# A one-core decoder layer: feed-forward loads begun at the end of the attention scores, their first splits ahead of the last output product's, token transposes further back

## The chip, the cores and the metric

The kernel runs on one core of a Trainium2 chip. The metric is the time of the program on the device in microseconds (us). Before the change three runs took 573.92 to 576.64 us, with a median of 574.91.

The engines of the core are TensorE (PE in the profile, its weight loads PEld), VectorE (DVE), ScalarE (ACT), GpSimd (POOL) and SyncE (SP). Each works through its own list of instructions in order, and semaphores tie the lists together. Transfers are issued from the lists of SP and POOL; those that add to what lies in memory are issued from POOL.

## The reference

One decoder layer on 512 tokens of width 1024, in float32: a norm, one input projection, three groups of heads (dilated attention with 6 heads, gated linear attention with 4, block-sparse attention with 6), an output projection with a residual, a second norm, a feed-forward part of width 4096 with a squared ReLU and a residual, and a final norm.

```python
def hybrid_layer(x, norm1_w, w_in, w_a2, b_a, gla_norm_w, w_out, norm2_w, w_ff1, w_ff2, rel_bias):
    Bsz, S, _ = x.shape
    h = rmsnorm(x, norm1_w)
    proj = h @ w_in
    aq, ak, av, bq, bk, bv, br, ba, cq, ck, cv = jnp.split(proj, list(np.cumsum(IN_SIZES)[:-1]), axis=-1)
    ...
    y_a = dilated_attention(heads(aq, A_HEADS), heads(ak, A_HEADS), heads(av, A_HEADS), bias_a)
    y_b = gla(heads(bq, B_HEADS), heads(bk, B_HEADS), heads(bv, B_HEADS), br, ba, w_a2, b_a, gla_norm_w)
    y_c = moba_attention(heads(cq, C_HEADS), heads(ck, C_HEADS), heads(cv, C_HEADS), bias_c)
    mix = jnp.concatenate([y_a.reshape(Bsz, S, A_WIDTH), y_b, y_c.reshape(Bsz, S, C_WIDTH)], axis=-1)
    x = x + mix @ w_out

    h2 = rmsnorm(x, norm2_w)
    x = x + jnp.square(jax.nn.relu(h2 @ w_ff1)) @ w_ff2
    return x

def reference(x, norm1_w, w_in, gla_w_a2, gla_b_a, gla_norm_w, w_out, norm2_w, w_ff1, w_ff2, rel_bias, final_norm_w):
    for i in range(DEPTH):
        x = hybrid_layer(x, norm1_w[i], w_in[i], gla_w_a2[i], gla_b_a[i], gla_norm_w[i], w_out[i],
                         norm2_w[i], w_ff1[i], w_ff2[i], rel_bias)
    return rmsnorm(x, final_norm_w)
```

With 512 tokens and blocks of 256, the block-sparse heads attend to all past keys, so both attention groups end as full causal scores with their own biases and masks.

## The kernel before, in words

**Arithmetic.** A float32 weight tile `wraw` (128 x 1024, 512 KB) is split in two: `wh`, rounded to the format that TensorE multiplies fast (a copy on ACT), and `wl`, the rest (a subtraction on DVE). Activations are split in the same way. A product is then three matmuls: high by high, high by low, low by high.

**Block products.** The output projection and the feed-forward matrices are multiplied in 2 x 2 blocks by seven block products instead of eight (numbers 0 to 6, executed in the order 0, 1, 3, 5, 2, 4, 6). Products 0 and 1 take blocks as they are; the others take sums and differences of blocks. Their results gather in accumulators X (0, 2, 4, 6), Y (1) and Z (3, 5). Each product of the output projection has two halves of 128 tokens (q = 0, 1) with 12 matmuls of 512 columns each. Each product of a feed-forward unit has two halves of 24 matmuls of 256 columns. There are four chunks of the hidden width, each with a unit for w_ff1 (accumulators f1X, f1Y, f1Z) and one for w_ff2 (f2X, f2Y, f2Z).

**Sums of weights.** The blocks of weights that a product needs are summed on the way in: a plain transfer from SP brings one block, and an adding transfer from POOL (`o_plus`, `plus`) puts the next on top. A product's buffer is often the buffer of an earlier product with one more block, and then the add has to wait until the earlier product's split has read it.

**Stages.** Projections and gated linear attention come first, then scores, softmax (`P`), transposes of `P` (`ptp`, `turn`) and values (`po`) by pairs of heads. As values end, `mix_out` splits them and makes the sums that the output projection multiplies (`ms`, `mh`, `ml`). `out_proj` runs the seven products; `o_add` adds each to the residual `x3` on DVE. When both halves of the width of a tile of 128 tokens are there (tiles 0 and 1 after product 2, tiles 2 and 3 after product 6), `x2_done` makes the reciprocal of the norm (`junk`, `m`, `tmp`, `y`), `y_out` scales the tile (`y0`), transposes it on TensorE (`yps`, eight 128 x 128 transposes in two accumulator banks), and scales it into `yf`; `y_parts` forms sums (`ys`) and splits (`yp`), which are the operands of the first feed-forward unit.

**What sets the order.** Every part is a Python generator (a stream) that hands out one instruction at a time. `Plan.run` keeps its own estimate of each engine's time and, of all streams, issues the instruction that could start first; ties go by the stream's priority (`prio`, the lower number first). ("take", name) and ("give", name) count buffers: `big` is a buffer of 4 KB a partition, `w` the right to split one more weight pair, `raw`, `rawo` and `raw2` the rights to load. ("wait", key) and `fire(key)` tie streams. What comes out is a fixed list for each engine; the waits on the chip then follow from the data. So an edit of one stream's rights shifts the order of others too.

In the kernel before, `fetch_o` loads product 6 of the output projection as a sum of its own: for each of its two weight tiles (ip = 0, 1) one plain transfer and three adding ones. `fetch_ff` and `cut_ff`, which load and split the feed-forward's weights, start when the last score transposes have been planned, and `cut_ff` waits until all of the output projection's splits have been planned ("o cut"). The first unit's splits are done in halves of 512 columns.

Of the kernel before, what the change touches and what calls it, by code (L numbers as in the profile page):

```python
# [100 lines left out]
class Plan:  # L101
# [48 lines left out]
    def run(self):  # L150
        while self.streams:
            cand, moved = None, False
            for st in list(self.streams):
                while True:
                    if st["item"] is None:
                        try:
                            moved = True
                            self.now = st["sent"] if st["sent"] is not None else st["at"]
                            st["item"] = st["gen"].send(st["sent"])
                        except StopIteration:  # L160
                            self.streams.remove(st)
                            break
                    it = st["item"]
                    if isinstance(it, tuple):
                        kind, key = it
                        if kind == "prio":
                            st["prio"] = key
                        elif kind == "wait":
                            if key not in self.done:
                                break  # L170
                            st["at"] = max(st["at"], self.done[key])
                        else:
                            if not self.free[key]:
                                break
                            t = min(self.free[key])
                            self.free[key].remove(t)
                            st["at"] = max(st["at"], t)
                        st["sent"], st["item"] = st["at"], None
                        continue
                    o = self.best(st)  # L180
                    first = o[0] if isinstance(o, list) else o
                    t = max(self.start(x, st["at"]) for x in (o if isinstance(o, list) else [o]))
                    if cand is None or (t, st["prio"], st["n"]) < cand[:3]:
                        cand = (t, st["prio"], st["n"], st, o)
                    break
            if cand is None:
                if moved:
                    continue
                if self.streams:
                    raise RuntimeError("streams wait for ever")  # L190
                return
            t, _, _, st, o = cand
            end = 0.0
            for x in o if isinstance(o, list) else [o]:
                end = max(end, self.issue(x, t))
            st["item"], st["sent"] = None, end
# [3 lines left out]
def hybrid_block_kernel(ctx: ExitStack, tc: tile.TileContext, xT_d, x_d, w0_d, wv_d, wqk_d, wo_d, w1_d, w2_d,  # L200
# [220 lines left out]
                fire(("x3", t, half))  # L421

    def fetch_o():
        for n, q, more in ((0, (0, 0), None), (1, (1, 0), None), (5, (1, 1), None), (4, (0, 1), ((1, 1),)),
                           (6, (1, 0), ((0, 0), (0, 1), (1, 1)))):
            for ip in range(2):
                yield ("take", "rawo")
                yield ("take", "big")
# [6 lines left out]

    def cut_o():
        for n in O_ORDER:
            for ip in range(2):
                yield ("wait", ("oB", n, ip))
                t = VB["o", n, ip]  # L440
                yield from parts(("o", n, ip), t)
                if n in (0, 3):
                    spawn(o_plus(2 if n else 3, ip, t, ((1 if n else 0, 1),)), 3)
                else:
                    give("rawo")
                    give("big")

        fire("o cut")

    XS = {}  # L450
    units = [(i, c) for c in range(NC) for i in (1, 2)]
# [106 lines left out]
            yield ("take", "w")  # L558

    def cut_ff():  # L560
        yield ("wait", "o cut")
        for u in units:
            for o, (n, *_) in enumerate(PRODUCTS):
                if u == units[0] or u == units[1]:
                    yield ("prio", 0.5 if u == units[0] else 3)
                if u == units[-1]:
# [671 lines left out]
    def y_out(t, half, y):  # L1238
        y0 = slot("y0")
        yield Any(DVE.tensor_scalar(y0, x3[t, half], y, None, op0=OP.mult), ACT.activation(y0, x3[t, half], AF.Copy, scale=y))  # L1240
        r = "og"[half] if t % 2 else "pt"
        yield ("take", r)
        pt = bank(r, "yps")
# [63 lines left out]
    def out_proj():  # L1307
# [39 lines left out]
        for n in O_ORDER:  # L1347
            if n == 1:
                yield ("wait", "scores")
                for q in range(2):  # L1350
                    yield from part(n, q, (0, 1, 2))
                yield ("wait", "turns")
                for q in range(2):
                    yield from part(3, q, (0, 1, 2))
                spawn(fetch_ff(), 4)
                spawn(cut_ff(), 3)
                spawn(y_parts(), 0.4)
            for q in range(2):
                yield from part(n, q, (3,) if n in (1, 3) else (0, 1, 2, 3))
            give_w()  # L1360
            give_w()
            if n in (2, 3):
                give("big")
                give("big")
            if n == 2:
                give("w")
                give("w")
            give("raw2")

    hq = {}  # L1370
# [343 lines left out]
```

## Time and profile before

| | before |
|---|---|
| median of 3 runs | 574.91 us (573.92 to 576.64) |
| the profiled execution | 574.53 us, span 572.8 us |
| PE busy | 555.9 us, 97% of the span |
| DVE busy | 480.9 us, 84% |
| ACT busy | 372.4 us, 65% |
| POOL busy | 71.1 us, 12% |
| bytes moved | 99.73 MB, 173 GB/s over the span |
| mean granted clock of TensorE | 0.996 |
| output projection on TensorE | 191.4 to 244.8 us |
| first feed-forward unit begins | 245.0 us |

Reading it: the profiled execution took 574.53 us in all, 1.7 us more than its span from the first to the last instruction. Matmuls on TensorE overlap, so its busy time is not its work; what tells of a loss is an idle time before an instruction and what ended it. An engine off the critical path may idle at no cost.

### The profile page before, as it was taken

The page shows a single profiled execution, that of the slowest core. Times are in us where ns is not written, and L with a number is a line of the kernel's source. Part 1 is how long each engine was busy: PE and PEld are TensorE (multiplying, and loading weights), DVE is VectorE, ACT ScalarE, POOL GpSimd, SP SyncE. Part 2 cuts the span into 40 slices and gives each one's busy share as a digit, 9 for nine tenths or more (in the row PEclk, how much of TensorE's full clock was granted, in tenths as well). Part 3 has the DMA queues.
Part 4 walks back from the last instruction along what each step waited for, and adds up shares of the span by engine and source line. Part 5 has one row for each costly group of instructions (what it writes and reads, how often), then busy time and mean ns, then how long its engine had stood idle before and what let it go on. Part 6 is the DMA issues. An engine that isn't in the chain of part 4 may idle for free.

```text
span 572.8 us, 9467 instructions
## 1 busy us (share of the span) xinstructions
PE 555.9 (97%) x3513; PEld 478.6 (84%) x3513; DVE 480.9 (84%) x879; ACT 372.4 (65%) x662; POOL 71.1 (12%) x93
## 2 busy tenths in 40 slices
PE   9999999999999999998999999999999999999994
PEld 8977887886786767788988899988999888999883
DVE  5899899977876988799799996799967799867993
ACT  6755644795865775788785466855467655579543
POOL 4012110001011011101212002020020110112101
PEclk9999999999999999999999999999999999999998
DMA  8944694396087549965988529787278594395812
GB/s 287 405 116 114 112 239 107 111 376 124 5 165 195 153 119 271 243 213 129 229 241 166 171 95 243 239 147 217 92 160 278 133 195 157 96 215 112 147 54 94
DMA packets 30813, 99.73 MB, mean 174 GB/s; under 512 B 3744, under 2 KB 3786, under 8 KB 30768
## 3 DMA queue, kind: packets, MB, share of 16 engines
q0 software_dynamic: 10032, 35.62, 34.4%
q1 hardware_dynamic: 20448, 63.25, 31.7%
q8 instruction: 27, 0.44, 0.3%
q10 hardware_dynamic: 288, 0.27, 0.1%
q14 instruction: 18, 0.15, 0.1%
HBM read 97.00 MB, written 2.13 MB: 173 GB/s over the span
## 4 chain that ended last, share of the span: by engine, by line
PE 85%; DVE 8%; ACT 3%; issue 1%; DMA 1%; SPq 0%; DVEq 0%; ACTq 0%
PE f2X L129 15%; PE f1X L129 15%; PE qkps L129 11%; PE f2Z L129 8%; PE f1Z L129 7%; PE vps L129 6%; PE ops L129 4%; PE f2Y L129 4%; PE f1Y L129 3%; PE sps L129 2%; PE po L129 2%; PE ptp L129 2%; DVE wl L129 2%; PE av L129 1%; DVE yf L129 1%; PE lp L129 1%
## 5 line engine op out<-in xcount | busy, mean ns | idle before, releaser
L129 DVE TENSOR_TENSOR wl<-wraw,wh 128x1024 fp32r<-128x1024 f32 (+2 forms) x174 | 191.3, 1109 | 36.0 <-ACT wh L129 35.8
L129 ACT ACTIVATE wh<-wraw 128x1024 fp32r<-128x1024 f32 (+2 forms) x173 | 164.3, 965 | 54.7 <-DVE x L129 9.7
L129 PE MATMUL f1X<-yp,wh 128*128 128x256 f32 x512 | 92.7, 283 | 0.0
L129 PEld LDWEIGHTS f1X<-yp,wh 128*128 128x128 f32 x512 | 80.1, 192 | 0.3
L129 POOL DMA_DIRECT2D wraw<-in_w x46 | 40.4, 952 | 273.8 <-DVE wl L129 205.2
L129 PE MATMUL f1X<-yp,wl 128*128 128x256 f32 x256 | 72.4, 283 | 0.0
L129 PE MATMUL f2X<-wh,Al 128*128 128x512 f32 (+1 forms) x132 | 50.5, 383 | 0.0
L129 PE MATMUL f2X<-wh,Ah 128*128 128x512 f32 (+1 forms) x132 | 50.5, 383 | 0.0
L129 PE MATMUL f2X<-wl,Ah 128*128 128x512 f32 (+1 forms) x132 | 50.5, 383 | 0.0
L129 PEld LDWEIGHTS f1X<-yp,wl 128*128 128x128 f32 x256 | 49.1, 192 | 0.0
L129 PE MATMUL f1Z<-yp,wh 128*128 128x256 f32 x256 | 46.3, 283 | 0.0
L129 PE MATMUL qkps<-xh,wh 128*128 128x512 f32 x96 | 40.8, 425 | 1.6 <-DVE vals L129 1.2
L129 ACT ACTIVATE h<-h 128x512 f32<-128x512 f32 x56 | 34.7, 625 | 11.5 <-DVE h L129 11.0
L129 PEld LDWEIGHTS f1Z<-yp,wh 128*128 128x128 f32 x256 | 39.9, 192 | 0.0
L129 ACT ACTIVATE Ah<-h 128x512 fp32r<-128x512 f32 x40 | 24.2, 620 | 22.2 <-DVE h L129 22.2
L129 PE MATMUL f1Z<-yp,wl 128*128 128x256 f32 x128 | 36.4, 284 | 1.8 <-DVE wl L129 1.8
L129 PE MATMUL qkps<-xh,wl 128*128 128x512 f32 x96 | 37.6, 392 | 0.0
L129 PE MATMUL qkps<-xl,wh 128*128 128x512 f32 x96 | 37.5, 391 | 0.0
L129 ACT ACTIVATE P<-P,mn 128x512 f32<-128x512 f32 (+3 forms) x48 | 26.5, 554 | 14.3 <-DVE mn L129 14.1
L129 PEld LDWEIGHTS f2X<-wl,Ah 128*128 128x128 f32 x132 | 24.8, 188 | 4.8
L129 PEld LDWEIGHTS f2X<-wh,Al 128*128 128x128 f32 x132 | 24.8, 188 | 4.8
L129 PEld LDWEIGHTS f2X<-wh,Ah 128*128 128x128 f32 x132 | 24.8, 188 | 4.7
(261 smaller groups left out, 1229.9 us busy)
## 6 DMA issues: line engine op xcount, KB each, us to landing
wraw<-in_w SPq DMA_DIRECT2D x66, 512.0 KB, 5.7
wraw<-in_w POOLq DMA_DIRECT2D x46, 512.0 KB, 6.4
wraw<-in_wqk SPq DMA_DIRECT2D x12, 512.0 KB, 6.5
wraw<-in_wo POOLq DMA_DIRECT2D x12, 512.0 KB, 7.4
wraw<-in_wv SPq DMA_DIRECT2D x10, 512.0 KB, 7.1
wraw<-in_wo SPq DMA_DIRECT2D x10, 512.0 KB, 6.2
wraw<-in_wv POOLq DMA_DIRECT2D x8, 512.0 KB, 5.8
nb<-tab SPq DMA_DIRECT2D x12, 256.0 KB, 4.8
```

Of the source, the lines that this page charges most:

```text
L129: getattr(getattr(self.nc, op.eng), op.method)(*op.args, **op.kw)
```

## The change

Four things change.

- `fetch_o` no longer loads product 6. In `cut_o`, product 2's buffer, once split, gets block (1, 0) added and becomes product 6's (`o_plus(6, ...)`), as product 0's already became product 3's and product 3's product 2's.
- `fetch_ff` and `cut_ff` are started as soon as the scores are planned, ahead of product 1. `cut_ff` waits for the split of output product 4 before it splits feed-forward product 0, and for that of output product 6 before feed-forward product 3. So the splits of feed-forward products 0 and 1 may come ahead of product 6's, which has the priority 0.4.
- Two rights to split (`w`) are given back after the last score transposes, not after product 2.
- The planner learns an item ("delay", t), which moves a stream's own earliest time on by t in the planner's estimate and issues nothing. `y_out` uses it with 2.0 between the scaled tile and its transposes.

```diff
--- before.py
+++ after.py
@@ -165,6 +165,8 @@
                         kind, key = it
                         if kind == "prio":
                             st["prio"] = key
+                        elif kind == "delay":
+                            st["at"] += key
                         elif kind == "wait":
                             if key not in self.done:
                                 break
@@ -421,8 +423,7 @@
                 fire(("x3", t, half))
 
     def fetch_o():
-        for n, q, more in ((0, (0, 0), None), (1, (1, 0), None), (5, (1, 1), None), (4, (0, 1), ((1, 1),)),
-                           (6, (1, 0), ((0, 0), (0, 1), (1, 1)))):
+        for n, q, more in ((0, (0, 0), None), (1, (1, 0), None), (5, (1, 1), None), (4, (0, 1), ((1, 1),))):
             for ip in range(2):
                 yield ("take", "rawo")
                 yield ("take", "big")
@@ -435,17 +436,19 @@
 
     def cut_o():
         for n in O_ORDER:
+            if n == 6:
+                yield ("prio", 0.4)
             for ip in range(2):
                 yield ("wait", ("oB", n, ip))
                 t = VB["o", n, ip]
                 yield from parts(("o", n, ip), t)
-                if n in (0, 3):
-                    spawn(o_plus(2 if n else 3, ip, t, ((1 if n else 0, 1),)), 3)
+                if n in (0, 3, 2):
+                    m, q = {0: (3, (0, 1)), 3: (2, (1, 1)), 2: (6, (1, 0))}[n]
+                    spawn(o_plus(m, ip, t, (q,)), 3)
                 else:
                     give("rawo")
                     give("big")
-
-        fire("o cut")
+            fire(("o cut", n))
 
     XS = {}
     units = [(i, c) for c in range(NC) for i in (1, 2)]
@@ -558,9 +561,10 @@
             yield ("take", "w")
 
     def cut_ff():
-        yield ("wait", "o cut")
         for u in units:
             for o, (n, *_) in enumerate(PRODUCTS):
+                if u == units[0] and o in (0, 2):
+                    yield ("wait", ("o cut", 6 if o else 4))
                 if u == units[0] or u == units[1]:
                     yield ("prio", 0.5 if u == units[0] else 3)
                 if u == units[-1]:
@@ -1238,6 +1242,7 @@
     def y_out(t, half, y):
         y0 = slot("y0")
         yield Any(DVE.tensor_scalar(y0, x3[t, half], y, None, op0=OP.mult), ACT.activation(y0, x3[t, half], AF.Copy, scale=y))
+        yield ("delay", 2.0)
         r = "og"[half] if t % 2 else "pt"
         yield ("take", r)
         pt = bank(r, "yps")
@@ -1347,13 +1352,15 @@
         for n in O_ORDER:
             if n == 1:
                 yield ("wait", "scores")
+                spawn(fetch_ff(), 4)
+                spawn(cut_ff(), 3)
                 for q in range(2):
                     yield from part(n, q, (0, 1, 2))
                 yield ("wait", "turns")
+                give("w")
+                give("w")
                 for q in range(2):
                     yield from part(3, q, (0, 1, 2))
-                spawn(fetch_ff(), 4)
-                spawn(cut_ff(), 3)
                 spawn(y_parts(), 0.4)
             for q in range(2):
                 yield from part(n, q, (3,) if n in (1, 3) else (0, 1, 2, 3))
@@ -1362,9 +1369,6 @@
             if n in (2, 3):
                 give("big")
                 give("big")
-            if n == 2:
-                give("w")
-                give("w")
             give("raw2")
 
     hq = {}
```

On TensorE, where product 2 of the output projection ends and product 4 runs, the first token tile's transposes stood here before (`ops_2354` and `ops_2492` are the two halves of accumulator X):

```order
L129 MATMUL ops_2492<-wl_2726,ms_2186 128x512
L129 MATMUL ops_2354<-wh_2732,ms_2196 128x512
L129 MATMUL ops_2354<-wh_2732,ms_2198 128x512
L129 MATMUL ops_2354<-wl_2733,ms_2196 128x512
L129 MATMUL yps_2807<-cst_80,y0_2804 128x128 x4
L129 MATMUL yps_2809<-cst_80,y0_2805 128x128 x4
```

and now stand here, with `ops_2386` and `ops_2461` as the two halves:

```order
L129 MATMUL ops_2386<-wl_2740,ms_2185 128x512
L129 MATMUL ops_2461<-wh_2724,ms_2184 128x512
L129 MATMUL ops_2461<-wh_2724,ms_2186 128x512
L129 MATMUL ops_2461<-wl_2725,ms_2184 128x512
...
L129 MATMUL yps_2837<-cst_80,y0_2831 128x128 x4
L129 MATMUL yps_2840<-cst_80,y0_2832 128x128 x4
```

The transposes moved from behind the first 3 matmuls of product 4 to behind 18 of its 24. Those of the second tile stood behind 15 matmuls of product 4 and now stand behind all of it and six of product 6.

On DVE, at the same place, before (`x3` is the residual, `wraw_2120` product 6's first weight tile):

```order
L129 TENSOR_TENSOR wl_2759<-wraw_2120,wh_2758 128x1024
L129 TENSOR_TENSOR x3_2142<-x3_2142,ops_2354 128x512
L129 SCALAR_TENSOR_TENSOR m_2689<-ssq_2785,m_2689 128x1
L129 SCALAR_TENSOR_TENSOR tmp_2794<-y_2793,m_2689 128x1
L129 SCALAR_TENSOR_TENSOR y_2793<-tmp_2794,y_2793 128x1
L129 TENSOR_SCALAR y0_2804<-x3_2132,y_2793 128x512
L129 TENSOR_TENSOR x3_2146<-x3_2146,ops_2492 128x512
```

and now (`wraw_2535`, `wraw_2537` and `wraw_2539` are feed-forward weights, `wraw_1616` is product 2's buffer, now product 6's):

```order
L129 TENSOR_TENSOR wl_2754<-wraw_2535,wh_2753 128x512 x2
L129 TENSOR_TENSOR x3_2152<-x3_2152,ops_2386 128x512
L129 TENSOR_TENSOR wl_2775<-wraw_2537,wh_2774 128x512 x2
L129 SCALAR_TENSOR_TENSOR m_2683<-ssq_2784,m_2683 128x1
L129 TENSOR_TENSOR wl_2752<-wraw_1616,wh_2751 128x1024
L129 SCALAR_TENSOR_TENSOR tmp_2799<-y_2798,m_2683 128x1
L129 TENSOR_TENSOR x3_2156<-x3_2156,ops_2461 128x512
L129 SCALAR_TENSOR_TENSOR y_2798<-tmp_2799,y_2798 128x1
L129 TENSOR_TENSOR wl_2806<-wraw_2539,wh_2805 128x512
L129 TENSOR_SCALAR y0_2831<-x3_2142,y_2798 128x512
```

Four half splits of feed-forward product 0 moved to both sides of product 2's first add, and product 6's first split and one more half split moved into the chain that makes the first tile's factor.

Further on, on DVE, where the first feed-forward unit's third product (number 3) gets its operand `yp`, before:

```order
L129 TENSOR_TENSOR wl_3071<-wraw_2696,wh_3070 128x512
L129 TENSOR_TENSOR ys_3099<-yf_3012,yf_3023 128x512
L129 TENSOR_TENSOR ys_3100<-yf_3013,yf_3024 128x512
L129 TENSOR_TENSOR wl_3071<-wraw_2696,wh_3070 128x512
L129 TENSOR_TENSOR yp_3114<-ys_3099,yp_3112 128x512
L129 TENSOR_TENSOR wl_3125<-wraw_2706,wh_3124 128x512
```

and now:

```order
L129 TENSOR_TENSOR wl_3107<-wraw_2777,wh_3106 128x512
L129 TENSOR_TENSOR ys_3142<-yf_3073,yf_3079 128x512
L129 TENSOR_TENSOR ys_3143<-yf_3074,yf_3080 128x512
L129 TENSOR_TENSOR h_3016<-h_3016,f1Y_3095 128x512
L129 TENSOR_TENSOR yp_3155<-ys_3142,yp_3153 128x512
```

`wraw_2696` and `wraw_2706` are the two weight tiles of product 3, `wraw_2777` is the second one of product 5. Before, product 3's second tile was split behind its operand; now product 3's splits and three of product 5's four half splits stand ahead of it.

## The prediction

> **What bounds the kernel now.** I read the page first, then the waits of TensorE, then its timeline round each wait, then the busy time of the engines stage by stage.
>
> ```profile
> span 572.8 us, 9467 instructions
> PE 555.9 (97%) x3513; PEld 478.6 (84%) x3513; DVE 480.9 (84%) x879; ACT 372.4 (65%) x662; POOL 71.1 (12%) x93
> ```
>
> TensorE (PE) is busy for 555.9 of 572.8 us, and the change takes no matmul away. So the question is only which of its gaps close, and which open.
>
> ```profile
> PE yps L129 <- DVE y L129: 2.2, 3, 1.2
> PE f1Z L129 <- DVE wl L129: 1.8, 2, 1.4
> PE ops L129 <- DVE x L129: 1.0, 1, 1.0
> PE ops L129 <- DVE mn L129: 0.3, 1, 0.3
> ```
>
> These are all its named waits from 200 us to 275 us (total, times, longest): the token transposes (yps), the second product on bank Z of the first feed-forward unit (f1Z), and two in the output projection (ops). In the timeline the idle time stands in brackets:
>
> ```profile
> 218.59 0.39 PE L129 MATMUL ops<-wl,ms 128*128 128x512 f32 x1
> 219.95 0.73 PE L129 MATMUL ops<-wh,ms 128*128 128x512 f32 x2 [0.97 <-DVE x L129]
> ...
> 235.04 0.39 PE L129 MATMUL ops<-wl,ms 128*128 128x512 f32 x1
> 236.63 1.06 PE L129 MATMUL yps<-cst,y 128*128 128x128 f32 x8 [1.20 <-DVE y L129]
> 237.45 0.71 PE L129 MATMUL ops<-wh,ms 128*128 128x512 f32 x2
> ...
> 250.75 0.28 PE L129 MATMUL f1X<-yp,wl 128*128 128x256 f32 x1
> 251.56 1.09 PE L129 MATMUL yps<-cst,y 128*128 128x128 f32 x8 [0.54 <-DVE y L129]
> ```
>
> ```profile
> 267.68 0.38 PE L129 MATMUL f1Z<-yp,wl 128*128 128x256 f32 x1 [0.40 <-DVE wl L129]
> 268.25 0.40 PE L129 MATMUL f1Z<-yp,wh 128*128 128x256 f32 x2
> 270.08 0.38 PE L129 MATMUL f1Z<-yp,wl 128*128 128x256 f32 x1 [1.44 <-DVE wl L129]
> ```
>
> Matmuls overlap, so what a wait costs is the distance of two starts less the ordinary step. The chain of waits, in order of time, gives the steps: 51 in 11.86 us, so 0.23 each in the projection, and 53 in 6.36, so 0.12 in the feed-forward.
>
> ```profile
> 219.95 11.86 PE ops L129 x51
> 267.02 0.60 DVE wl L129
> 268.23 1.20 DVE yf L129 x2
> 273.69 6.36 PE f1X L129 x53
> ```
>
> Then 219.95 lost 1.36 - 0.23 = 1.13, 236.63 lost 1.59 - 0.23 = 1.36, 251.56 lost 0.81 - 0.12 = 0.69, and 270.08 lost 1.83 - 0.24 = 1.59 (two matmuls start at 268.25). The smaller ones, from their brackets with the same 0.15 on top, are 0.3 (the projection's wait on mn), 0.6 (the transposes of the third token tile) and 0.55 (267.68). Together 6.2 us: that is all there is to win here. The last row above runs on unbroken; TensorE shows no wait from there to the end.
>
> What sets these waits is VectorE (DVE) with ScalarE (ACT) beside it:
>
> ```profile
> 225.00:230.00 5.00, 5.00 (x24) 4.14 (x23) 3.46 (x5) 0.72 (x2) 1.75 (x2) 1.00 0.97 221
> 230.00:235.00 5.00, 5.00 (x27) 4.16 (x27) 3.17 (x11) 2.77 (x8) 0.00 (x0) 1.00 1.06 283
> 240.00:245.00 5.00, 5.00 (x23) 4.14 (x23) 5.00 (x11) 4.74 (x11) 0.88 (x1) 1.00 1.03 172
> 260.00:265.00 5.00, 5.00 (x44) 5.00 (x43) 5.00 (x10) 4.30 (x9) 0.88 (x1) 1.00 0.93 234
> ```
>
> Columns: the stretch, then PE, its weight loads, DVE, ACT, POOL, the granted clock, the DMA share, GB/s. From 225 to 235 DVE idles for 3.4 of 10 us and ACT for 6.5; from 240 on DVE is full. DVE work brought forward from the second stretch into the first is worth its time; a mere exchange of places within the second is worth nothing by itself.
>
> **The change, part by part.** Times below are on the clock of the trace of before.
>
> *Fewer transfers for product 6.* Two plain and four adding transfers of w_out go (six of 512 KB). Nothing in the list above waits for them: worth 0 directly. Behind it stands a new chain: product 6's weights are now product 2's buffer plus one block, so its add starts only when DVE has made product 2's wl.
>
> *Attention's tail.* TensorE's order has three matmuls moved from ahead of the last values product (po) to behind it. So its result comes 3 x 0.23 = 0.7 us earlier for the same work, and the DVE chain behind it (ml, mixes, adds) had been waiting for it. The loss at 219.95 falls from 1.13 to about 0.4, and the 0.3 on mn should go, since more matmuls now cover it: +1.0. It is 0 if the reordered attention ahead opens a gap of that size: there a score step needs DVE's last split of k, and by my count it has 0.4 us in hand.
>
> *The transposes.* Tile 0 now stands 18 matmuls behind product 2 instead of 3, tile 1 30 instead of 15 (apart from the transposes), tiles 2 and 3 some 2 to 3 us further back too. On DVE its chain gets longer, since splits stand inside it:
>
> ```profile
> 226.47 1.22 DVE L129 TENSOR_TENSOR wl<-wraw,wh 128x1024 fp32r<-128x1024 f32 x1
> 228.44 0.69 DVE L129 TENSOR_TENSOR x<-x,ops 128x512 f32<-128x512 f32 x1 [0.75 <-PE ops L129]
> 229.92 0.16 DVE L129 SCALAR_TENSOR_TENSOR m<-ssq,m 128x1 f32<-128x1 f32 x1 [0.79 <-ACT junk L129]
> 232.28 0.61 DVE L129 TENSOR_SCALAR yf<-yps,nw 128x128 f32<-128x128 f32 x2 [0.17 <-PE yps L129]
> ...
> 234.43 0.35 DVE L129 TENSOR_SCALAR yf<-yps,nw 128x128 f32<-128x128 f32 x1 [0.43 <-ACT yf L129]
> ```
>
> Product 2's first add stays at 228.4. Behind it come two half splits of feed-forward product 0 (0.60 each, as the wl row of the chain), product 6's first split (1.13, waiting for ACT's 1.0), the second add, one more half split and two scalings (0.4 each): 228.4 + 0.6 + 1.2 + 0.6 (ACT) + 1.2 + 0.6 + 0.6 + 0.2 + 0.8 = 234.2. TensorE reaches tile 0 at 219.95 + (48 + 18) x 0.23 = 235.1: no wait. Tile 1 is behind product 6's second split and the eight yf of tile 0, which DVE and ACT hand to and fro for 2.4 us (232.28 to 234.70 above): ready at about 239.2, while TensorE arrives at 235.1 + 0.85 (236.63 to 237.45, eight transposes) + 12 x 0.23 = 238.7. Lost 0.6 instead of 1.36. Tiles 2 and 3: ready 0.4 us or more ahead, 1.3 won.
>
> *Feed-forward product 0 (f1X).* It had found its operands ready. Now TensorE comes to it at 239.2 + 0.85 + 18 x 0.23 = 244.2, and DVE, between tile 1's scaling and the first yp, has an add, four half splits, another add, yp itself (7 x 0.60 = 4.2) and five yf with ACT's share in between (2.3): 239.2 + 6.5 = 245.7. A new wait of 1.5. Bounds: 0 if the hand-offs are quicker or the scalings come earlier, 2.5 if each hand-off costs 0.2 more.
>
> *Products 3 and 5 (f1Z).* The half splits of product 5 now stand ahead, so the 2.15 there (0.55 + 1.59) falls to about 0.2. The price: five half splits and one h more (3.6 us) lie ahead of the first yp of product 3. From 245.7 DVE needs some 13 us of work and 1.2 of waits for ACT to that yp: 259.8; TensorE arrives at 245.7 + 96 x 0.12 + 2 x 0.85 = 258.9. A new wait of 0.8 (0 to 2).
>
> **Sum.** Lost before 6.2; lost after 0.4 + 0 + 0.6 + 0 + 1.5 + 0.8 + 0.2 = 3.5. Gain 2.7 us, and as TensorE is then unbroken to the end, it keeps it. The profiled execution had 574.53 us for its span of 572.8, and is 0.4 below the runs' median of 574.91. So 571.8 on its own scale, and **572.2** as a median.
>
> **Where transfers decide.** Product 6's two adds are issued at about 221.4 and 223.3 (0.5 behind their splits, which end 220.9 and 222.8).
>
> ```profile
> wraw<-in_wo POOLq DMA_DIRECT2D x1, 512.0 KB, 7.2
> ...
> wraw<-in_wo POOLq DMA_DIRECT2D x1, 512.0 KB, 8.0
> ```
>
> ```profile
> 207.75 2.68 POOL L129 DMA_DIRECT2D wraw<-in_wo  x3 [11.15 <-ACT th L129]
> 223.95 0.87 POOL L129 DMA_DIRECT2D wraw<-in_wo  x1 [13.53 <-DMA wraw<-in_wo]
> ```
>
> Adds at 207.75 and 223.95 took 7.2 and 8.0 us to land (the transfers by window). The third of the three from 207.75, issued at 209.5, released the next only at 223.95: 14.4. With 8 the first lands at 229.4, and ACT wants it at 229.8: just in time. I take 8, as it is the row with one add and feed-forward loads beside it. The Trainium skill's page "DMA: Bandwidth & Descriptors" (section on the anatomy of a GpSimd DMA) fits 2.0 us plus bytes over 436 GB/s, which for 512 KB is 3.2; these rows disagree, and by it the sum would be the same with 5 us to spare.
>
> **The rivals.**
> (B) *All the waits go and none comes.* For it: ACT and DVE idle 9.9 us of two engines' 20 from 225 to 235, and the hand-offs may be shorter than in my count. Against it: DVE is full from 240. Then 6.2 - 0.4 is won: 574.5 - 5.8 + 0.4, about 569.1.
> (C) *DVE bounds the stretch whatever its order.* The gaps only move: f1X waits 2.5 and f1Z 2.5. For it: 5.00 of 5 busy. Against it: the 2.4 us of feed-forward splits that go into DVE's idle time. The gain is 2.7 - 2.7 = 0: 574.9.
> (D) *Slower: product 6's first add lands late and holds ACT and DVE, which take their work in order.* At 13 to 14 us, as the third one did, it lands at 234.4 to 235.4 instead of 229.8. Then the scalings of tile 0, queued behind it on DVE, are 4.6 to 5.6 late, TensorE waits some 4 at the transposes, and everything behind shifts. It decides against the change from a landing time of about 11 us, where the 2.7 are used up. For it: a DMA share near 1.0 there. Against it: it is first in its queue, and six transfers fewer. 572.2 + 4.6 to 5.6 is 576.8 to 577.8, and over that with a late second add. The Trainium skill's page "TensorE: Matmul & The Clock Gate" (section on HAM oscillation) says that gaps over some 3.4 us bring the clock to half; no row here shows it (the clock is 1.00 in all rows above, the longest gap 1.44), and by it this rival would cost about 1.7 us more, an estimate from that page.
> (E) *The delay does nothing:* not so; the order of TensorE shows the transposes further back.
>
> **How the numbers follow.** My forecast 0.48 (its own range 570.7 to 573.8), B 0.21, C 0.14, D 0.17. Half a per cent, 2.9 us, is about what a measurement tells from no change, so the line is at 572.0: half of the forecast's cases and nearly all of B lie below it (0.24 + 0.20 = 0.44 faster); D lies above 577.8 in 0.10, C in 0.02 (0.12 slower); the rest, 0.44, is within. For 8 in 10 the range runs from 569.2 (half of B left out) to 576.4 (most of D left out).
>
> **What would show it.** Right: in the waits of TensorE no f1Z on wl; one yps wait, on tile 1, under 1 us; new waits of f1X and of f1Z on yp; eight adding and eight plain transfers of w_out; product 6's splits on ACT without an idle time before them; DVE busier from 225 to 235. Wrong: an idle time of ACT ahead of wh that ends with a DMA (D); no wait for yp (B); waits before 200 us (then the attention's reorder is what I mis-sized).

## The result, and the profile after

The changed kernel took 571.67 us (median of 4 runs, 570.97 to 572.49) against 575.12 for the kernel before beside it (573.92 to 576.64): a ratio of 0.9936, 95% interval 0.9913 to 0.9958. Timed again in five rounds it took 572.28 against 574.73, 0.9958 (0.9944 to 0.9972). So it is some 2.4 to 3.5 us faster; 572.2 was predicted. One execution of a kernel below, of the one without the delay, took 686.97 us at a granted clock of 0.75 and is left out of its ratio.

The page of the changed kernel, with its span and engines, and its output projection's transfers:

```profile
span 570.7 us, 9458 instructions
PE 556.3 (97%) x3513; PEld 477.9 (84%) x3513; DVE 479.0 (84%) x875; ACT 373.6 (65%) x666; POOL 67.8 (12%) x89
...
wraw<-in_wo SPq DMA_DIRECT2D x8, 512.0 KB, 6.2
wraw<-in_wo POOLq DMA_DIRECT2D x8, 512.0 KB, 5.9
```

TensorE's named waits from 180 to 280 us (total, times, longest), and the same places in its timeline:

```profile
PE f1Y L129 <- DVE yf L129: 1.2, 1, 1.2
PE f1X L129 <- DVE x L129: 0.8, 1, 0.8
PE ops L129 <- DVE x L129: 0.2, 1, 0.2
PE f1X L129 <- DVE yp L129: 0.2, 1, 0.2
```

```profile
219.83 0.39 PE L129 MATMUL ops<-wl,ms 128*128 128x512 f32 x1
220.45 0.73 PE L129 MATMUL ops<-wh,ms 128*128 128x512 f32 x2 [0.23 <-DVE x L129]
...
238.94 0.39 PE L129 MATMUL ops<-wl,mh 128*128 128x512 f32 x1
239.48 1.06 PE L129 MATMUL yps<-cst,y 128*128 128x128 f32 x8
...
244.26 0.39 PE L129 MATMUL ops<-wl,mh 128*128 128x512 f32 x1
245.41 0.35 PE L129 MATMUL f1X<-yp,wh 128*128 128x256 f32 x1 [0.76 <-DVE x L129]
245.92 0.39 PE L129 MATMUL f1X<-yp,wh 128*128 128x256 f32 x1 [0.15 <-DVE yp L129]
...
252.41 0.28 PE L129 MATMUL f1X<-yp,wl 128*128 128x256 f32 x1
253.87 0.51 PE L129 MATMUL f1Y<-yp,wh 128*128 128x256 f32 x2 [1.18 <-DVE yf L129]
```

By the prediction's measure (distance of two starts less the ordinary step) the gaps are 0.39 at 220.45, 0.31 at the transposes of tile 1 (239.48), 0.92 + 0.39 = 1.31 ahead of the first feed-forward product, and 1.46 - 0.12 = 1.34 ahead of the second (f1Y); two jumps of 0.16, one of them shortly ahead of the last values product, have no name. Together some 3.7 us, where 6.2 stood before. Both waits of f1Z on wl are gone, and eight plain and eight adding transfers of w_out are left, as announced.

VectorE's work did move into its idle time. The stretches from 225 to 235 us (columns as in the prediction):

```profile
225.00:230.00 5.00, 5.00 (x24) 4.14 (x23) 4.32 (x7) 2.17 (x5) 1.35 (x2) 1.00 1.06 211
230.00:235.00 5.00, 5.00 (x24) 4.14 (x23) 4.54 (x11) 4.23 (x10) 0.00 (x0) 1.00 1.04 256
```

DVE was busy for 6.63 of these 10 us and is now for 8.86, ACT for 3.49 and now for 6.40.

Where the 2.0 us between the two profiled spans (572.75 and 570.71) came from can be cut in three. TensorE executes 1179 matmuls from the first score step (sps) to the first f2X, in both kernels; this stretch is called **the middle** from here on. Its ends, before:

```profile
96.69 0.97 PE L129 MATMUL sps<-k,q 64*128 64x512 f32 x6
...
290.81 0.40 PE L129 MATMUL f2X<-wh,Ah 128*128 128x512 f32 x1
```

and after:

```profile
97.59 0.97 PE L129 MATMUL sps<-k,q 64*128 64x512 f32 x6
...
289.63 0.40 PE L129 MATMUL f2X<-wh,Ah 128*128 128x512 f32 x1
```

The middle fell from 194.12 to 192.04, by 2.08 us. The start was 0.90 longer in this one execution; in the repeat of the same kernel the first score step stood at 96.58, so that is chance. From the first f2X to ScalarE's last instruction both took 277.28. And from there to the last instruction, **the end**, it went from 4.66 to 3.80. So +0.90 - 2.08 - 0.86 = -2.04. The repeat had a middle of 192.13 and an end of 3.91.

### The profile page after: what moved, and what is told of

The parts are those of the page before. It is cut to its first block, busy times and chain, and to the rows that moved or that the text cites. A ratio compares the mean times of both kernels' runs of the same rounds, so it can differ in the third digit from the quotient of the medians.

```text
span 570.7 us, 9458 instructions
## 1 busy us (share of the span) xinstructions
PE 556.3 (97%) x3513; PEld 477.9 (84%) x3513; DVE 479.0 (84%) x875; ACT 373.6 (65%) x666; POOL 67.8 (12%) x89
## 4 chain that ended last, share of the span: by engine, by line
PE 88%; DVE 6%; ACT 3%; issue 1%; DMA 1%; SPq 0%; DVEq 0%; ACTq 0%
PE f2X L129 15%; PE f1X L129 15%; PE qkps L129 11%; PE f1Z L129 8%; PE f2Z L129 8%; PE vps L129 6%; PE f1Y L129 4%; PE f2Y L129 4%; PE ops L129 3%; PE sps L129 3%; PE ptp L129 2%; PE po L129 2%; DVE wl L129 1%; PE av L129 1%; PE lp L129 1%
## 5 line engine op out<-in xcount | busy, mean ns | idle before, releaser
L129 DVE TENSOR_TENSOR Al<-h,Ah 128x512 fp32r<-128x512 f32 x40 | 26.7, 685 | 3.4 <-ACT Ah L129 3.4
```

The source lines that it names most:

```text
L129: getattr(getattr(self.nc, op.eng), op.method)(*op.args, **op.kw)
```

## The experiments

Since the gains are near what a median can tell, each profile is read by its middle and its end, beside the ratio. There is one profile of each kernel; where the same order on TensorE was profiled twice, the two middles agreed within 0.1 us (192.04 and 192.13 for the change). All ratios are to the kernel before in the same session.

```
kernel                        early  new p6  delay   middle    end   ratio (95% interval)
before                          -      -       -     194.12   4.66   1
the change                     yes    yes     2.0    192.04   3.80   0.9936 (0.9913 to 0.9958)
the change again               yes    yes     2.0    192.13   3.91   0.9958 (0.9944 to 0.9972)
without the delay              yes    yes      -     191.45   3.80   0.9935 (0.9919 to 0.9950)
without product 6's edit       yes     -      2.0    191.95   4.67   0.9961 (0.9947 to 0.9974)
without the early loads         -     yes     2.0    194.30   3.95   0.9987 (0.9977 to 0.9997)
early loads alone              yes     -       -     192.88   3.87   0.9972 (0.9956 to 0.9987)
delay alone                     -      -      2.0    195.02   3.69   0.9995 (0.9985 to 1.0005)
product 6's edit alone          -     yes      -     195.27   4.69   1.0022 (1.0010 to 1.0035)
early loads, late splits     loads    yes     2.0    199.29   3.80   1.0073 (1.0058 to 1.0088)
delay of 1.0                   yes    yes     1.0    190.46   3.80   0.9923 (0.9908 to 0.9937)
delay of 1.5                   yes    yes     1.5    190.38   3.80   0.9912 (0.9892 to 0.9932)
```

Between the middle and the end lie 277.28 or 277.29 us in all of these but two: 277.72 with the delay alone and 278.18 with early loads and late splits. The early return of the two rights to split, the third part of the change, goes with the early loads, with one exception: the kernel without the early loads still has it.

Theory 1 is the prediction's: each edit closes or opens gaps of TensorE, and they can be summed. Theory 2 is its rival C: VectorE is full, and waits only move.

**The change again** (no edit).

> The changed kernel once more, in more rounds, for the size of the gain. The two profiled executions differ by 2.1 us between the first score step and the second feed-forward unit; their starts differ by 0.9 us (the changed one later, waiting for its first loads) and their last output transfers by 0.9 the other way. Theory 1 (the gain is TensorE's gaps, 6.2 us lost before and about 3.7 after, less 0.6 for a busier attention order): 2 to 2.5 us faster, ratio 0.9956 to 0.9965. Theory 2 (fewer transfers also shorten the start or the end, so the 3.45 us of the medians are real): ratio 0.9940 or lower, and a start and an end that are shorter in this profile too.

The ratio lies in theory 1's range, and the start is not shorter. But the end is, by 0.75, so theory 2 of this run holds a part: a program's end is treated below.

**Without the delay**, on the changed kernel:

```diff
-        yield ("delay", 2.0)
```

> Only the 2.0 us of delay ahead of the transposes is taken out; the rest of the change stays. Theory 1 (each wait is worth its gap): the transposes wait for y again, 1.0 to 1.4 us at tile 1 and 0.3 to 0.7 at the later tiles, while the waits of the first feed-forward product (1.3) and of the second (1.2) shrink by half at most: 1 to 2 us slower than the changed kernel, ratio to the kernel before 0.998 to 1.000. Theory 2 (VectorE's order of work bounds the stretch and the waits only move along TensorE): the sum of the waits stays at 3.7 within 0.5, ratio as the changed kernel's.

The transposes wait again, as theory 1 said; the two rows of the waits are these:

```profile
PE yps L129 <- DVE y L129: 1.8, 2, 1.2
PE ops L129 <- DVE x L129: 0.2, 1, 0.2
```

But the waits of f1X and f1Y are gone altogether, not by half: the middle is 0.6 shorter than with the delay. Theory 1 had the sign wrong; the waits moved and their sum fell. In this setting the delay of 2.0 is a loss.

**Without product 6's edit**, on the changed kernel:

```diff
-        for n, q, more in ((0, (0, 0), None), ..., (4, (0, 1), ((1, 1),))):
+        for n, q, more in ((0, (0, 0), None), ..., (4, (0, 1), ((1, 1),)),
+                           (6, (1, 0), ((0, 0), (0, 1), (1, 1)))):
...
-            if n == 6:
-                yield ("prio", 0.4)
...
-                if n in (0, 3, 2):
-                    m, q = {0: (3, (0, 1)), 3: (2, (1, 1)), 2: (6, (1, 0))}[n]
-                    spawn(o_plus(m, ip, t, (q,)), 3)
+                if n in (0, 3):
+                    spawn(o_plus(2 if n else 3, ip, t, ((1 if n else 0, 1),)), 3)
```

> Only product 6's weights are made as before (a plain load and three adding transfers a half) and their split's place in the queue with it; early feed-forward loads and delay stay. Theory 1: attention's order is that of before again, the waits of the output projection on mn and x come back (0.3 and 1.1), the 0.6 of the busier attention order goes: 0.5 to 1 us slower than the changed kernel, ratio 0.997 to 0.998. Rival (the three adds in a row, beside feed-forward loads that now start earlier, land late, and ScalarE waits at product 6's splits): 4 us slower or more, with an idle time of ScalarE ahead of wh that ends with a DMA.

The middle is 191.95, the same as with the edit, so theory 1's 0.5 to 1 is not there, and no add landed late either: the last one of w_out landed at 226.1 us. The waits of the projection came back in part (0.3 on mn, 0.4 on x), two new ones of 0.2 to 0.3 came (m, wl), and the shorter attention, treated under "Attention's tail" below, paid for them.

**Without the early loads**, on the changed kernel:

```diff
-                spawn(fetch_ff(), 4)
-                spawn(cut_ff(), 3)
...
+                spawn(fetch_ff(), 4)
+                spawn(cut_ff(), 3)
                 spawn(y_parts(), 0.4)
...
-                if u == units[0] and o in (0, 2):
-                    yield ("wait", ("o cut", 6 if o else 4))
+                if u == units[0] and o == 0:
+                    yield ("wait", ("o cut", 6))
```

> Feed-forward loads and splits are begun where they were before (behind the turns, and behind all of the output projection's splits); product 6's new weights and the delay stay. Theory 1: the third and fourth product's waits on wl come back (0.55 and 1.6), the first product's wait for yp (1.3) falls to 0.3 or less: 0.5 to 1.5 us slower than the changed kernel, ratio 0.997 to 0.999. Theory 2 (order does not matter where VectorE is full): no difference to the changed kernel, the same sum of waits at other places.

The waits on wl are back:

```profile
PE f1Z L129 <- DVE wl L129: 2.3, 2, 1.2
PE yps L129 <- DVE m L129: 0.9, 1, 0.9
PE f1Z L129 <- DVE yp L129: 0.7, 1, 0.7
```

The middle is 194.30, not shorter than before's: all of the gain in the middle hangs on this edit, more than theory 1 gave it, and against theory 2.

**Early loads alone**, on the kernel before:

```diff
                 yield ("wait", "scores")
+                spawn(fetch_ff(), 4)
+                spawn(cut_ff(), 3)
...
                 yield ("wait", "turns")
+                give("w")
+                give("w")
...
-        yield ("wait", "o cut")
...
+                if u == units[0] and o in (0, 2):
+                    yield ("wait", ("o cut", 6 if o else 4))
```

> The kernel before with the early feed-forward loads and splits alone (their start at the end of the scores, the first splits ahead of product 6's, and the two buffers given back earlier); product 6's weights as before, no delay. By the runs so far, from the first score step (sps) to the first f2X matmul TensorE took 194.1 us before and 192.0 in the changed kernel, 191.5 without the delay, 192.0 without product 6's edit, and 194.3 without the early loads. If the early loads are the whole gain, as these say: 191.4 here (2.7 less than before), and an end as before's, 4.66 us from ScalarE's last instruction: ratio 0.995 to 0.996, no f1Z wait on wl. If they only work together with product 6's edit (its adds queue behind the loads): ScalarE waits for a transfer at product 6's splits, and the time is that of before or more.

The middle is 192.88: 1.24 gained alone, not the 2.7 that adding up gives; no wait on wl is left at f1Z, and no transfer is waited for, so neither expectation holds whole. (The old places of the moved lines are not shown above.) What replaces the waits is one wait at the last tile's transposes:

```profile
PE yps L129 <- DVE y L129: 1.9, 1, 1.9
```

**Early loads, late splits**, on the changed kernel:

```diff
-                if u == units[0] and o in (0, 2):
-                    yield ("wait", ("o cut", 6 if o else 4))
+                if u == units[0] and o == 0:
+                    yield ("wait", ("o cut", 6))
```

> The changed kernel, its feed-forward loads as early as there, but the splits of all feed-forward products behind all of product 6's. If the gain is VectorE's work brought into its idle time (the splits): the f1Z waits come back in part, 1 to 2 us, and sps to f2X is 193 to 194. If it is the earlier transfers alone: 192.0 as in the changed kernel.

It is the splits and not the transfers: with the loads as early but the splits behind, f1Z waits 5.0 us for wl in four waits, far more than expected. TensorE's rows there, and its clock (the column behind POOL) round them:

```profile
260.62 0.39 PE L129 MATMUL f1Z<-yp,wl 128*128 128x256 f32 x1 [1.31 <-DVE wl L129]
...
264.23 0.38 PE L129 MATMUL f1Z<-yp,wl 128*128 128x256 f32 x1 [2.63 <-DVE wl L129]
...
266.06 0.58 PE L129 MATMUL f1Z<-yp,wl 128*128 128x256 f32 x1 [0.83 <-DVE wl L129]
```

```profile
225.00:230.00 5.00, 5.00 (x24) 4.14 (x23) 2.25 (x4) 1.00 (x3) 0.69 (x1) 1.00 1.03 218
...
256.00:266.00 10.00, 4.92 (x35) 4.08 (x33) 10.00 (x18) 7.54 (x14) 0.88 (x1) 0.95 0.47 107
...
260.00:265.00 5.00, 1.75 (x12) 1.54 (x12) 5.00 (x9) 4.70 (x10) 0.88 (x1) 1.00 0.54 95
265.00:270.00 5.00, 4.17 (x20) 3.94 (x19) 5.00 (x9) 4.43 (x9) 0.88 (x1) 0.50 0.55 86
```

From 225 to 230 DVE works 2.25 us where it works 4.32 in the changed kernel: these 2.1 us of splits then stand in the full stretch (10.00 of 10 from 256 to 266), ahead of TensorE. And after 5 us in which TensorE was busy for 1.75 the clock was 0.50, from 265.0 to 271.8. The 27 matmuls from 266.06 to 271.94 took 5.88 us, where 27 steps of 0.12 are 3.24: 2.6 us more. This kernel's middle is also 5.0 longer than that of the one without early loads, whose splits are as late. By TensorE's steps 2.6 of it is the clock and some 2.3 are longer waits (8.0 us lost against 5.6). Why the waits are longer isn't settled; its VectorE list has parts of later operands (yp) ahead of the wl that f1Z waits for.

**Delay alone**, on the kernel before:

```diff
+        yield ("delay", 2.0)
         r = "og"[half] if t % 2 else "pt"
```

> The kernel before with the 2.0 us of delay ahead of the transposes alone. My working of the prediction (a transpose further back loses its wait): the yps waits of 1.36, 0.6 and 0.69 shrink to 0.6 in all, sps to f2X 192 to 193. The rival that the run without delay speaks for (VectorE is full behind 240 us, so a later transpose delays its yf, the yp and the splits behind them): no gain or a loss of up to 0.7, 194.1 to 194.8, with new waits at f1X for yp and at f1Y for yf.

The middle is 195.02, 0.90 longer: the rival, and a bit beyond its range. The transposes' wait fell to 0.8 from 2.2, and f1X now waits for splits that stand behind:

```profile
PE f1X L129 <- DVE wl L129: 1.9, 4, 0.7
PE ops L129 <- DVE x L129: 1.0, 1, 1.0
PE f1Z L129 <- DVE wl L129: 0.9, 1, 0.9
```

That the ratio is nevertheless 1 within its interval goes with the end, 0.97 shorter in this profile.

**Product 6's edit alone**, on the kernel before:

```diff
-                if n in (0, 3):
-                    spawn(o_plus(2 if n else 3, ip, t, ((1 if n else 0, 1),)), 3)
+                if n in (0, 3, 2):
+                    m, q = {0: (3, (0, 1)), 3: (2, (1, 1)), 2: (6, (1, 0))}[n]
+                    spawn(o_plus(m, ip, t, (q,)), 3)
```

with its load of its own taken out and the splits' priority as in the change.

> The kernel before with product 6's new weights alone (product 2's buffer plus one block, its splits' place in the queue); loads, splits and transposes of the feed-forward as before. From sps to the first f2X matmul TensorE took 194.1 us before, 192.9 with the early loads alone, 195.0 with the delay alone, 192.0 with both, 194.3 with the delay and this edit, 191.5 with the early loads and this edit. If the edits add up: this edit is worth between -1.4 (as beside the early loads) and +0.1 (as beside both), 192.7 to 194.2. If it only makes room for the early loads, nothing by itself: 194.1 or more. The projection's waits on x and mn shrink from 1.4 to 0.4 in either case, and the busier attention order costs 0.6.

By itself it is a loss of 1.15, outside the adding-up range. The planner put the new splits late, and TensorE, which is at product 6 by then, waits for both parts of the second one, for wh and then for wl. The view names m, a tiny instruction behind wl on VectorE, as the second releaser; but wl ended at 242.60 and m only at 242.67, and TensorE went on at 242.66:

```profile
241.14 0.50 PE L129 MATMUL ops<-wh,mh 128*128 128x512 f32 x1 [0.43 <-ACT wh L129]
...
242.66 0.50 PE L129 MATMUL ops<-wl,mh 128*128 128x512 f32 x1 [0.78 <-DVE m L129]
```

```profile
241.38 1.22 DVE L129 TENSOR_TENSOR wl<-wraw,wh 128x1024 fp32r<-128x1024 f32 x1
242.52 0.15 DVE L129 TENSOR_SCALAR m<-ssq 128x1 f32<-128x1 f32 x1
```

So this edit costs 1.15 alone, is worth 1.43 beside the early loads (192.88 to 191.45), 0.72 beside the delay (195.02 to 194.30) and nothing beside both. The delay costs 0.90 alone and 0.6 beside the other two, and is worth 0.93 beside the early loads and 0.97 beside product 6's edit. The early loads gain in all four settings: 1.24, 3.07, 3.82 and 2.2. Three of these numbers hold the early return of the rights to split too; the 2.2, beside both other edits, doesn't. The 0.72 and the 0.97 compare a kernel without that return with one that has it, so they don't belong to the named edit alone; the rights weren't tried by themselves. The other numbers of product 6's edit and of the delay show without these that edits of this planner's streams don't add up; only the sign of the early loads, with the rights, is firm.

**The length of the delay**, on the changed kernel:

```diff
-        yield ("delay", 2.0)
+        yield ("delay", 1.0)
```

and the same with 1.5.

> The changed kernel with 1.0 us of delay in place of 2.0. If the cost of the delay grows with its length: sps to f2X between 191.5 (none) and 192.0 (2.0). If there is a best length, at which neither the transposes nor the first products wait: below 191.4, ratio 0.992 or lower.

> The changed kernel with 1.5 us of delay in place of 2.0. From sps to f2X: 191.45 with no delay, 190.46 with 1.0, 192.1 with 2.0. If there is a best length near 1: 190.5 to 192 here, ratio 0.992 to 0.994, with part of the transposes' waits of 1.0 (1.05 and 0.41) gone and part of the waits of f1X and f1Y of 2.0 (1.3 and 1.2) back. If the length only picks one of several orders without a trend: anything from 190 to 193.

Both lengths give the same list of instructions on TensorE, VectorE and ScalarE, and so are two timings of one program, a middle of 190.4 to 190.5 and a ratio of 0.991 to 0.992: the best of all tried, 1.6 us shorter in the middle than the changed kernel. At 1.0 the transposes wait a little and no feed-forward product waits at all:

```profile
PE yps L129 <- DVE y L129: 1.1, 2, 0.9
PE ops L129 <- DVE x L129: 0.2, 1, 0.2
```

With 0, 1.0 and 2.0 the middle is 191.45, 190.46 and 192.1: there is a best place for the transposes. A trend within that is not shown, as 1.5 is no program of its own.

**A late add for product 6**, on the changed kernel:

```diff
+        if (n, ip) == (6, 0):
+            nc.gpsimd.dma_start(t, wo_d[qs[0][0], qs[0][1], ip], accum_op=OP.add)
         for q in qs:
             yield POOL.dma_start(t, wo_d[q[0], q[1], ip], accum_op=OP.add)
```

> The changed kernel in which the first half of product 6's weights gets its last block added twice, so that its second add starts only when the first has landed; every engine's order but GpSimd's is the same. (The added block is counted twice there, so that half's weights are other numbers; no work is left out.) It prices the prediction's slower rival. The first half then lands at about 233 us instead of 227.3, ScalarE wants it at 230.3, the second half at about 234 instead of 229.7. Theory D (ScalarE and VectorE hold everything queued behind): ScalarE idles 2 to 3 us ahead of wh, ended by a DMA; TensorE waits 1.5 to 3 us more at the transposes or the first product, 1.5 to 3 us slower than the changed kernel, ratio about 1.000. If a late add is covered: ratio as the changed kernel's, 0.994 to 0.996.

The ratio was 1.0038 (1.0019 to 1.0057). The added half landed at 235.2 and the other at 239.0, later than expected. ScalarE's row at the split, TensorE's at its gap, and the stretches behind it:

```profile
235.27 1.06 ACT L129 ACTIVATE wh<-wraw 128x1024 fp32r<-128x1024 f32 x1 [5.71 <-DMA wraw<-in_wo]
```

```profile
238.36 1.04 PE L129 MATMUL ops<-wh,ms 128*128 128x512 f32 x2 [4.85 <-DVE x L129]
```

```profile
238.40:241.90 3.50, 3.50 (x11) 2.83 (x12) 3.12 (x6) 2.58 (x7) 0.00 (x0) 0.53 1.08 215
242.00:246.00 4.00, 4.00 (x25) 3.31 (x23) 2.97 (x11) 3.01 (x7) 0.00 (x0) 1.00 0.76 150
```

Theory D holds, at a higher price than the 1.5 to 3 us expected: ScalarE's idle time ends with a transfer, VectorE waits for it, TensorE for VectorE. The gap lies ahead of product 4's second half and not at the transposes: that half waits for the add (x) which empties its accumulator, and the add stands behind the split on VectorE. The middle is 198.57, 6.5 more than the changed kernel's: 5.0 for the gap and 1.7 for the clock behind it (six matmuls in 2.54 us instead of 1.38, then eight transposes in 1.34 instead of 0.80), less the 0.3 that tile 1's transposes no longer wait.

**The end of the program**, on the kernel before:

```diff
         yield DVE.memset(eps, EPS)
+        pad = [small("pad", (128, 1)) for _ in range(3)]
+        for _ in range(8):
+            nc.vector.memset(pad[0], 0.0)
+            nc.gpsimd.memset(pad[1], 0.0)
+        for _ in range(8):
+            nc.scalar.activation(pad[2], eps, AF.Copy)
```

> The kernel before with eight tiny fills of a 128x1 tile on VectorE and on GpSimd and eight tiny copies on ScalarE at the very start, while all wait for the first loads; all else in the same order. In the profiles the program ends 4.66 us behind ScalarE's last instruction where a packet of instructions (queue 14) falls into the last output transfer, and 3.8 to 3.9 where it falls ahead of it. If the place of that packet goes by the count of instructions of one of these engines: the packet moves ahead, the end shrinks to 3.8 with sps to f2X unchanged at 194.1, ratio 0.998 to 0.999. If it is SyncE's or TensorE's, or goes by time: 4.66 as before, ratio 1.000.

The kernel before with 24 useless instructions more was faster: 573.46 against 574.51, a ratio of 0.9983 (0.9971 to 0.9996), with a middle of 194.19 and an end of 3.66. The transfers from the last output's issue to the end of the program, in the kernel before (queue, kind: packets, MB, share; then issues with the time to landing):

```profile
q10 hardware_dynamic: 144, 0.26, 15.5%
q14 instruction: 1, 0.01, 0.4%
...
out<-xw ACTq DMA_DIRECT2D x1, 256.0 KB, 3.7
```

and with the padding:

```profile
q10 hardware_dynamic: 144, 0.26, 19.0%
...
out<-xw ACTq DMA_DIRECT2D x1, 256.0 KB, 2.7
```

This last output is issued from ScalarE's list (ACTq). The packet of instructions that lay inside it before is not there. It was the same in every profile: where a q14 packet fell 2.15 us behind ScalarE's last instruction the end was 4.66 to 4.69 (before, without product 6's edit, product 6's edit alone), elsewhere 3.66 to 3.95. Which of the three engines' counts moved it wasn't tried, and how a packet that took some 0.3 us itself (0.4% of 16 engines' 4.7 us) delays the end by 0.8 to 1.0 isn't shown.

## Why the prediction was right, and where it was not

**The forecast** was 2.7 us less. Measured: 2.0 to 2.1 in the middle, and 0.8 at the end, which the prediction didn't have. So the total is nearer than the steps deserve, and that is luck: 0.6 was lost in one place and 0.8 found in another. The 0.8 goes with the place of a packet of instructions and not with the new order of work.

**Attention's tail.** The gap at 219.95 was to fall from 1.13 to 0.4: 0.39. The wait on mn was to go: gone. But the reorder has a price of 0.6 in which TensorE never waits. The last values product's first row, before and after:

```profile
210.94 0.97 PE L129 MATMUL po<-th,v 128*64 128x256 f32 x6
```

```profile
211.46 0.97 PE L129 MATMUL po<-th,v 128*64 128x256 f32 x6
```

From the first sps that is 675 matmuls in 114.25 us, and now 672 in 113.87. Three fewer at 0.23, and no 0.3 for mn, should have made 113.3. By the steps between neighbours no single place explains the 0.6: one jump of 0.16 is part of it, and TensorE goes 17 times instead of 14 from wide matmuls to the short ones of sps or po, at some 0.32 a step where a step among the wide ones takes 0.23; the rest is spread. The price belongs to product 6's edit: with the early loads and without that edit the same 672 matmuls took 113.54 and 113.58, in all kernels with it 113.87 to 113.95. The step "it is 0 if the reordered attention opens a gap of that size" looked for a gap, and a cost without one was not thought of.

**The transposes.** Tile 0 no wait: right. Tile 1 0.6: 0.31. Tiles 2 and 3 none: right. As a sum over gaps the step held; as a cause it didn't, since without the delay the middle is 0.6 shorter still. What was closed here was opened again, at f1X and f1Y.

**Product 0 (f1X).** 1.5 forecast, 1.31 measured, with the residual's add (x) and then yp as releasers, both in the list of VectorE that the step had counted. By the code the first of the two is a wait for a bank: f1X's accumulator has the tag "mm", which the add of product 6 gives back.

**Product 3 (f1Z), 0.8 for yp: the step that failed.** There was no such wait. Instead f1Y, the product before it, lost 1.34 to yf. Accumulator Y has the banks with the tag "pt", the same that the transposes of tiles 0 and 2 are written to (`r = "og"[half] if t % 2 else "pt"`), and they come free when yf has read them. Tile 2's transposes, moved back, stand only six matmuls ahead of f1Y, and VectorE is still reading them when TensorE gets there at 252.5:

```profile
253.46 0.87 DVE L129 TENSOR_SCALAR yf<-yps,nw 128x128 f32<-128x128 f32 x3 [0.44 <-ACT yf L129]
```

The other runs bear this out: in the kernels without product 6's edit and with the late add the distance is also six matmuls, and f1Y waits for 1.1 and 1.2; without the delay, with 1.0 of it, with the early loads or the delay alone, and before, at least 18 matmuls stand between, and f1Y doesn't wait. The prediction followed the operands to each product and not the banks; it lists every other wait at the right place.

**Product 5.** 2.15 to 0.2: 0.16. Right, and the reason given fits: its splits stand in time that had been idle, and in the run with early loads and late splits the waits on wl are back.

**Transfers.** Product 6's adds landed 5.4 and 6.0 us after their issue, at 227.3 and 229.7, not 8; ScalarE split the first at 230.29 without an idle time. Rival D was further off than "just in time", by some 3 us, and its price was right in kind: 4.6 to 5.6 late was to cost 4.6 to 5.6; 5.7 of idle time on ScalarE cost 5.0 in TensorE's gap, and the clock 1.7 on top. Here the rule cited from the Trainium skill, page "TensorE: Matmul & The Clock Gate" (section on HAM oscillation), that idle gaps over some 3.4 us bring the clock to half, has a row: a gap of 4.85 us, and 0.53 behind it. The 1.7 us estimated from that page agrees with the run; the section's own example has some 1.67 us throttled after each gap, of which half is lost, so less than here.

**Rival C** (VectorE bounds, gaps only move) is right for the delay and wrong for the early loads. The sentence ahead of the sum, that work brought into idle time counts and an exchange of places in the full stretch doesn't, fits what the early loads did in all four settings; the sum then gave 1.3 us to an exchange. **Rival B** (no new wait comes) came nearest with the delay at 1.0 and 1.5: medians of 570.18 and 570.24 us, where 569.1 was named for the change itself.

## What to carry to other kernels

Ask of each moved instruction whether it leaves a full stretch for an idle one; here that was the only move that gained in every setting. Where a wait is closed by putting the waiting work later, look for it again behind. For each place that TensorE is moved to, follow the accumulator's bank as well as the operands, and compare equal numbers of matmuls from end to end, since a new order can cost what no wait shows. Where edits act through a planner, test them in combinations and read the gain by stages of the trace, since the end of the program alone differed by up to 1 us here with no cause in the order of work.

## What was not expected of the hardware

- In the three profiles in which an 8 KB packet of instructions lay inside the last 256 KB output transfer, the program ended 0.7 to 1.0 us later than in the others (the transfer landed 3.7 us after issue in the kernel before, and 2.7 with the padding); 24 tiny instructions at the start took it away.
- The clock went to 0.50 at 265.0, for 6.8 us, after 5 us whose longest idle time was 2.63 us but in which TensorE was busy for only 1.75. The section on HAM oscillation in the Trainium skill's page "TensorE: Matmul & The Clock Gate" puts it at idle gaps over some 3.4 us; by this run two shorter ones, 1.31 and 2.63 us, close together do it too. The 4.85 us gap of the late add agrees with the page, with 0.53 over 3.5 us.
- An add of 512 KB landed in 5.4 to 6.0 us where 8.0 had been read off the kernel before, in stretches with the same DMA share near 1; the two of the late add's run took 8.6 and 11.5. The share doesn't tell the landing time.
